# Splitting the first norm's squares, the first gating and the bias rows' skewed copies differently in a two-layer decoder trunk

## The chip, the core and the metric
One core of one Trainium2 chip runs the whole program. The metric is the device time of one execution in microseconds; three runs of the kernel before gave 973.3, 973.38 and 974.68, median 973.38.

## What is computed
Two layers over x of 256 positions by 1024 channels, all in float32. Each layer is: a SwiGLU feed-forward block (hidden width 2816) added at half weight, a mixer (differential attention with a relative bias, a short gated convolution, a gated linear recurrence), and a second half-weight SwiGLU block; each starts from an RMS norm.

```python
def rms_norm(x, g, eps=RMS_EPS):
    y = xf * lax.rsqrt(jnp.mean(xf * xf, axis=-1, keepdims=True) + eps)
    return y * g
def swiglu(x, w_gate, w_up, w_down):
    return (jax.nn.silu(x @ w_gate) * (x @ w_up)) @ w_down
for l in range(DEPTH):
    h = x + 0.5 * swiglu(rms_norm(x, ffn1_norm[l]), ffn1_gate[l], ffn1_up[l], ffn1_down[l])
    ...                       # mixer; its attention adds bias = rel_bias[t5_bucket(q - k)]
    x = h + 0.5 * swiglu(rms_norm(h, ffn2_norm[l]), ffn2_gate[l], ffn2_up[l], ffn2_down[l])
return rms_norm(x, final_norm)
```

## The kernel before
**Weights.** SP loads the weights in pieces of 512 KB (tile `raw`, 6 buffers, L151). Each piece is split in two parts for TensorE: ACT writes the high part `wh` (L162), DVE the rest `wl` (L166); there are 7 buffers of each, so at most 7 pieces are ready ahead of PE. The helper `pump()` splits the next piece, `take(n)` hands ready pieces to PE, and `done(n)` frees them and starts their loads.

**A feed-forward block.** `up_gate` walks 11 units of 256 hidden columns. A unit is four pieces; each piece gives two rows of blocks (`na` and `nb`, one for each half of the positions), in 12 matmuls of three kinds (L204, L205, L206: high by high, low by high, high by low). After its four pieces a unit is gated (`gate`): ACT applies Silu into `sg` (L315, two instructions, scaled by the norm's reciprocal root `norm.r`), DVE multiplies into `ga` (L317, two). The gated unit is turned (`turn`) after the second piece of the next unit: PE transposes it into `hT` (L326, four), ACT takes the high part into `hid` (L328), DVE the low part (L329). Then come the down pieces, for four blocks n of output channels, each six pieces of eight pairs of matmuls (L221, L222; the last piece half as many), accumulating over the hidden units in order: the first five pieces of a block need units 0 to 9, the next unit 10. The turn of the last unit (`last()`) stands after the second down piece (k0 == 4).

**The norm.** It is applied late: the matmuls run on x times its gain, and `norm.r` enters at the gating. `Norm.ssq` sums the squares in `xq` over partitions on PE (L249); `start` makes the mean on DVE (L237), the power on POOL (L241) and two scaled identity matrices `dg` on DVE (L244), which only the mixer's `spread` reads. In the very first block the squares come from x itself (`first_squares`: two ACT squares into `junk`, L807, then three POOL adds, L808 to L810), placed after unit 0; ssq and the gating of unit 0 come after the second piece of unit 1, its turn after the fourth.

**Work hidden in the first block.** A table of hooks runs small pieces of preparation after the units 1, 2, 4, 5, 6, 7 and 9: loads of constants, bias rows (`bias_rows`: one matmul, and a copy into `br`, 8 partitions by 384 values), exponents, a softplus polynomial, factors. `skew_out` (unit 7, L457) writes `br` to a DRAM tile `skew`, each of the 8 rows 128 times over: one DMA on ACT's queue of 1024 rows of 1536 bytes, 1.5 MB. `skew_in` (unit 9, L461) reads it back, shifted by one place for each partition, into `bias` (128 partitions by 8 by 256, 1 MB), again from ACT's queue; ACT waits at that instruction until the first transfer has landed. The instructions of an engine run in the order in which the program was written.

Of the kernel before, what the change touches and what calls it, by code (L numbers as in the profile page):

```python
# [11 lines left out]
F32 = mybir.dt.float32  # L12
F32R = mybir.dt.float32r
AF = mybir.ActivationFunctionType
ALU = mybir.AluOpType
AX = mybir.AxisListType

P = 128
DEPTH = 2
S = 256  # L20
# [32 lines left out]
UNITS = KF // 2  # L53
# [17 lines left out]
def trunk(ctx: ExitStack, tc: tile.TileContext, t, out):  # L71
    nc = tc.nc
# [4 lines left out]
    wk = ctx.enter_context(tc.tile_pool(name="wk", bufs=2))  # L77
    sm = ctx.enter_context(tc.tile_pool(name="sm", bufs=4))
    ps = ctx.enter_context(tc.tile_pool(name="ps", bufs=8, space=bass.MemoryType.PSUM))
    dr = ctx.enter_context(tc.tile_pool(name="dr", bufs=1, space=bass.MemoryType.DRAM))  # L80

    def bank(name):
        return ps.tile([P, 512], F32, tag="bank", name=name)

    def pair(name):
        return [bank(name + "a"), bank(name + "b")]
# [18 lines left out]
    xq = cst.tile([P, S], F32, name="xq")  # L105
    ident = cst.tile([P, P], F32, name="ident")
    ones = cst.tile([P, P], F32, name="ones")
    bd = cst.tile([P, 2, DEPTH * 2, P], F32, name="bd")
    bias = cst.tile([P, 8, S], F32, name="bias")
# [89 lines left out]
    def done(n):  # L199
        st["done"] += n  # L200
# [7 lines left out]
    def col(o, w, i, vh, vl, ks, first=0, last=KD - 1):  # L208

        c = slice(i * P, (i + 1) * P)  # L210
        for k in ks:
            wh, wl = w[k // 4]
            mm3(o, wh[:, k % 4, c], wl[:, k % 4, c], vh[:, k], vl[:, k], k == first, k == last)
# [10 lines left out]
    def tok(k):  # L224
        return slice(k * P, (k + 1) * P)
# [8 lines left out]
    class Norm:  # L234
        def start(self, ssq):
            ms = sm.tile([P, 2], F32, tag="ms", name="ms")
            nc.vector.tensor_scalar(  # L237
                out=ms, in0=ssq, scalar1=1.0 / D, scalar2=RMS_EPS, op0=ALU.mult, op1=ALU.add
            )
            self.r = sm.tile([P, 2], F32, tag="rr", name="rr")  # L240
            nc.gpsimd.tensor_tensor(out=self.r, in0=ms, in1=mhalf[:, :2], op=ALU.pow)  # L241
            self.dg = wk.tile([P, 2, P], F32, tag="dg", name="dg", bufs=1)
            for k in range(2):
                nc.vector.tensor_scalar_mul(out=self.dg[:, k], in0=ident, scalar1=self.r[:, k:k + 1])  # L244

        def ssq(self):
            b = bank("ssq")
            for k in range(2):
                nc.tensor.matmul(  # L249
                    b[:, k:k + 1], lhsT=xq[:, k * P:(k + 1) * P], rhs=ones[:, 0:1], start=True, stop=True  # L250
                )
            self.start(b[:, 0:2])

        def spread(self):
            b = bank("rb")
# [42 lines left out]
    def up_gate(norm, first, hooks=()):  # L298

        hooks = dict(hooks)  # L300
        hid, tiles = [], []
        for j, n in enumerate((10, 8, 4)):
            tile_ = big.tile([P, n, 2, S], F32R, tag=f"A{j}", name=f"hid{j}")
            tiles.append((len(hid), tile_))
            hid += [tile_[:, k] for k in range(n)]

        def hidden(c):
            k0, tile_ = [x for x in tiles if x[0] <= 2 * c][-1]
            return tile_[:, 2 * c - k0:2 * c - k0 + 2]

        def gate(b):
            s = wk.tile([P, 2, 256], F32, tag="sg", name="sg")
            a = wk.tile([P, 2, 256], F32, tag="ga", name="ga")
            for k in range(2):
                nc.scalar.activation(out=s[:, k], in_=b[k][:, :256], func=AF.Silu, scale=norm.r[:, k:k + 1])  # L315
            for k in range(2):
                nc.vector.scalar_tensor_tensor(  # L317
                    out=a[:, k], in0=b[k][:, 256:], scalar=norm.r[:, k:k + 1], in1=s[:, k], op0=ALU.mult, op1=ALU.mult
                )
            return a  # L320

        def turn(c, a):
            b = bank("hT")
            for j in range(2):
                for k in range(2):
                    nc.tensor.transpose(b[:, (2 * j + k) * P:(2 * j + k + 1) * P], a[:, k, tok(j)], ident)  # L326
            h = hidden(c)
            nc.scalar.activation(out=h[:, :, 0], in_=two(b), func=AF.Copy)  # L328
            nc.vector.tensor_tensor(out=h[:, :, 1], in0=two(b), in1=h[:, :, 0].bitcast(F32), op=ALU.subtract)  # L329

        late = {}
        for c in range(UNITS):
            b = pair("n")
            if first and c == 0:
                start(b)
                first_squares()
            else:
                for j in range(4):
                    w = [None] * j + take(1)
                    if j < 3 or c > 0:  # L340
                        for k in range(2):
                            rows(b[k], w, k, (2 * j, 2 * j + 1))
                    else:
                        for k in range(2):
                            rows(b[k], w, k, (KD - 2,))
                        rows(b[0], w, 0, (KD - 1,))
                        norm.ssq()
                        rows(b[1], w, 1, (KD - 1,))
                    done(1)
                    if first and c == 1:  # L350
                        if j == 1:
                            norm.ssq()
                            late[0] = gate(b0)
                        if j == 3:
                            turn(0, late.pop(0))
                    elif j == 1 and c > 0:
                        turn(c - 1, late.pop(c - 1))
                    pump()
            if first and c == 0:
                b0 = b  # L360
            else:
                late[c] = gate(b)
            if c in hooks:
                hooks[c]()
        return hid, lambda: turn(UNITS - 1, late.pop(UNITS - 1))

    def ffn(norm, first, gain, hooks=()):
        hid, last = up_gate(norm, first, hooks)
        for n in range(4):
            acc = pair("d")  # L370
            for k0, k1 in DOWN_K:
                w = take(1)[0]
                for i in range(2):
                    c = slice(i * P, (i + 1) * P)
                    for k in range(k0, k1):
                        wide(acc[i], w[0][:, k - k0, c], w[1][:, k - k0, c], hid[k], k == 0, k == KF - 1)
                    if k1 == KF:
                        settle(2 * n + i, acc[i], gain, True)
                done(1)
                if n == 0 and k0 == 4:  # L380
                    last()
                pump()


    kept = {}
# [66 lines left out]
        kept["br"] = wk.tile([8, 384], F32, tag="at", name="br")  # L452
        nc.vector.tensor_copy(out=kept["br"], in_=b[:8, :384])

    def skew_out():
        kept["skew"] = dr.tile([8, P, 384], F32, name="skew")
        nc.scalar.dma_start(out=kept["skew"], in_=kept["br"].unsqueeze(1).to_broadcast([8, P, 384]))  # L457

    def skew_in():
        sk = kept["skew"][:]  # L460
        nc.scalar.dma_start(  # L461
            out=bias, in_=bass.AP(sk.tensor, sk.offset + P - 1, [[383, P], [P * 384, 8], [1, S]])
        )


    def mixer(l, norm):
# [180 lines left out]
            col(lxb[i][:, :S], w, i, xh, xl, range(KD - 1))  # L647
        col(lxb[0][:, :S], w, 0, xh, xl, (KD - 1,))
        norm.ssq()
        col(lxb[1][:, :S], w, 1, xh, xl, (KD - 1,))  # L650
        done(2)
        pump()
# [44 lines left out]
        for i in range(2):  # L697
            j = 2 * l + i
# [30 lines left out]
        for i in range(2):  # L729
            nc.vector.tensor_tensor_scan(  # L730
                out=tv[:, i], data0=av[:, i], data1=bx[:, i], initial=0.0, op0=ALU.mult, op1=ALU.add
# [8 lines left out]
        for i in range(2):  # L740
            nc.scalar.activation(
                out=cs[:, i], in_=cp[:, i, 2:], func=AF.Copy, scale=par("sc_conv_w", l * 6 + 4 + i)
# [61 lines left out]
    def first_squares():  # L804
        junk = big.tile([P, KD, S], F32, tag="A3", name="junk")
        for i in range(2):
            nc.scalar.activation(out=junk[:, 4 * i:4 * i + 4], in_=xT[:, 4 * i:4 * i + 4], func=AF.Square)  # L807
        nc.gpsimd.tensor_tensor(out=junk[:, 0:4], in0=junk[:, 0:4], in1=junk[:, 4:8], op=ALU.add)  # L808
        nc.gpsimd.tensor_tensor(out=junk[:, 0:2], in0=junk[:, 0:2], in1=junk[:, 2:4], op=ALU.add)
        nc.gpsimd.tensor_tensor(out=xq, in0=junk[:, 0], in1=junk[:, 1], op=ALU.add)  # L810

    norm = Norm()
    ffn(norm, True, ("mix_norm", 0), {1: constants_in, 2: bias_rows, 4: exponents, 5: softplus, 6: factors, 7: skew_out, 9: skew_in})
    for l in range(DEPTH):
        norm = Norm()
        mixer(l, norm)
        norm = Norm()
        if l < DEPTH - 1:
            ffn(norm, False, ("ffn1_norm", l + 1))
            norm = Norm()  # L820
# [13 lines left out]
    hid, turn_last = up_gate(norm, False, {2 + 2 * k + n: turn_back(k, n) for k in range(2) for n in range(2)})  # L834
# [43 lines left out]
    for d in range(KF - 4):  # L878
        w = take(1)[0]
        for k in range(2):  # L880
            for n in range(len(cuts[k])):
                row(k, n, w, d)
        done(1)
        if d == 4:
            turn_last()
        pump()
    w = take(4)
# [54 lines left out]
```

## Time and profile before

| | us |
|---|---|
| three runs | 973.3, 973.38, 974.68 |
| the profiled execution | 973.29, of it span 971.3 |
| PE busy | 955.9 (98%) |
| DVE, ACT, POOL busy | 584.8, 507.2, 26.6 |
| share of PE in the chain that ended last | 92% |
| share of the `skew` write in it | 4% |

A row of the timeline has its start, its duration and what it is; in brackets stands how long the engine had been idle before it, and what released it. [...] Busy times overlap, so they are not to be added; a matmul of 512 columns is shown with 0.39 us, but one starts 0.2275 us after the other.

### The profile page before, as it was taken

Reading aid. Unit: us, or ns where it says so; the run is one execution under the profiler, and the core shown is the slowest. Engines: PE = TensorE matmul, PEld = TensorE weight load, DVE = VectorE, ACT = ScalarE, POOL = GpSimd, SP = SyncE. Lnnn points to the kernel's source line nnn. Section 1 sums busy time; section 2 is a strip of 40 time slices with the busy share of each in tenths; the row PEclk is TensorE's granted clock in tenths of the full one; section 3 lists DMA queues with packets and bytes.
Section 4 is the critical chain, followed back from the end, with each engine's and each line's share of the span. In section 5 each row is a group of like instructions: output and inputs, shape, how many; then the busy total and the mean of one; then the engine's idle time right before and its main releaser. Section 6 shows DMA issues by size and latency. Waiting matters only on the chain.

```text
span 971.3 us, 13926 instructions
## 1 busy us (share of the span) xinstructions
PE 955.9 (98%) x5350; PEld 831.4 (86%) x5350; DVE 584.8 (60%) x817; ACT 507.2 (52%) x775; POOL 26.6 (3%) x49
## 2 busy tenths in 40 slices
PE   8899999999999999999999999999999999999997
PEld 7688877899999888888888888888999988888886
DVE  5666536667787555556655555565678765555543
ACT  6555435457775544444544445454678554444431
POOL 2003000000000000000000000000000000000000
PEclk9999999999999999999999999999999999999999
DMA  8575667554356555546555555556445465555531
GB/s 305 191 242 197 149 176 268 189 174 152 131 177 214 193 192 180 188 158 197 183 202 176 176 192 184 182 167 218 160 135 164 161 214 190 178 175 191 191 117 44
DMA packets 52997, 176.64 MB, mean 182 GB/s; under 512 B 6819, under 2 KB 8900, under 8 KB 52932
## 3 DMA queue, kind: packets, MB, share of 16 engines
q1 hardware_dynamic: 48960, 171.46, 51.8%
q10 hardware_dynamic: 3972, 4.29, 2.0%
q8 instruction: 42, 0.69, 0.3%
q14 instruction: 23, 0.19, 0.1%
HBM read 173.11 MB, written 2.62 MB: 181 GB/s over the span
## 4 chain that ended last, share of the span: by engine, by line
PE 92%; DMA 4%; ACT 1%; DVE 1%; issue 1%; SPq 0%; POOL 0%; ACTq 0%; POOLq 0%; DVEq 0%
PE na L205 8%; PE nb L204 8%; PE na L206 8%; PE nb L205 8%; PE nb L206 8%; PE na L204 8%; PE da L221 6%; PE db L221 6%; DMA skew<-br 4%; PE da L222 3%; PE db L222 3%; PE hT L326 2%; PE v L204 1%; PE wb L206 1%; PE wb L205 1%
## 5 line engine op out<-in xcount | busy, mean ns | idle before, releaser
L162 ACT ACTIVATE wh<-raw 128x1024 fp32r<-128x1024 f32 (+1 forms) x334 | 339.6, 1030 | 277.0 <-PE nb L206 106.9
L166 DVE TENSOR_TENSOR wl<-raw,wh 128x1024 fp32r<-128x1024 f32 (+1 forms) x334 | 390.8, 1194 | 80.0 <-ACT wh L162 80.0
L205 PE MATMUL na<-wl,xx 128*128 128x512 f32 x352 | 137.7, 391 | 4.8 <-DVE wl L166 4.8
L204 PE MATMUL na<-wh,xx 128*128 128x512 f32 x352 | 141.5, 402 | 0.5 <-ACT wh L162 0.5
L204 PE MATMUL nb<-wh,xx 128*128 128x512 f32 x352 | 137.9, 392 | 0.0
L206 PE MATMUL na<-wh,xx 128*128 128x512 f32 x352 | 137.7, 391 | 0.0
L206 PE MATMUL nb<-wh,xx 128*128 128x512 f32 x352 | 137.5, 391 | 0.0
L205 PE MATMUL nb<-wl,xx 128*128 128x512 f32 x352 | 137.5, 390 | 0.0
L329 DVE TENSOR_TENSOR hid<-hT,hid 128x512 fp32r<-128x512 f32 x44 | 30.4, 692 | 128.4 <-ACT hid L328 128.4
L221 PE MATMUL da<-hid,wh 128*128 128x512 f32 x252 | 93.6, 403 | 0.0
L221 PE MATMUL db<-hid,wh 128*128 128x512 f32 x252 | 92.3, 399 | 0.0
L205 PEld LDWEIGHTS na<-wl,xx 128*128 128x128 f32 x352 | 66.3, 188 | 18.0 <-DVE wl L166 5.9
L206 PEld LDWEIGHTS nb<-wh,xx 128*128 128x128 f32 x352 | 66.4, 189 | 14.1
L205 PEld LDWEIGHTS nb<-wl,xx 128*128 128x128 f32 x352 | 66.4, 189 | 14.0
L204 PEld LDWEIGHTS nb<-wh,xx 128*128 128x128 f32 x352 | 66.4, 189 | 14.0
L206 PEld LDWEIGHTS na<-wh,xx 128*128 128x128 f32 x352 | 66.2, 188 | 14.1
L204 PEld LDWEIGHTS na<-wh,xx 128*128 128x128 f32 x352 | 66.3, 188 | 13.4 <-ACT wh L162 1.4
L328 ACT ACTIVATE hid<-hT 128x512 fp32r<-128x512 f32 x44 | 26.2, 596 | 89.4 <-PE hT L326 89.4
L222 PE MATMUL da<-hid,wl 128*128 128x256 f32 x252 | 71.3, 283 | 0.0
L222 PE MATMUL db<-hid,wl 128*128 128x256 f32 x252 | 70.7, 281 | 0.0
L317 DVE SCALAR_TENSOR_TENSOR ga<-na,rr,sg 128x256 f32<-128x256 f32 x44 | 21.2, 483 | 73.8 <-ACT sg L315 73.8
L221 PEld LDWEIGHTS da<-hid,wh 128*128 128x128 f32 x252 | 47.9, 190 | 11.2
(283 smaller groups left out, 1523.2 us busy)
## 6 DMA issues: line engine op xcount, KB each, us to landing
raw<-in_ffn_gu SPq DMA_DIRECT2D x172, 512.0 KB, 4.4
raw<-in_ffn_down SPq DMA_DIRECT2D x82, 512.0 KB, 4.4
raw<-in_w_in SPq DMA_DIRECT2D x44, 512.0 KB, 4.6
raw<-in_w_out SPq DMA_DIRECT2D x16, 512.0 KB, 4.9
raw<-in_ffn_down SPq DMA_DIRECT2D x12, 256.0 KB, 2.7
raw<-in_ffn_gu SPq DMA_DIRECT2D x8, 256.0 KB, 5.0
skew<-br ACTq DMA_DIRECT2D x1, 1536.0 KB
xT<-in_x SPq DMA_DIRECT2D x4, 256.0 KB, 5.4
```

The source lines that it names most:

```text
L162: nc.scalar.activation(out=parts[i][0][:, s], in_=raws[i][:, s], func=AF.Copy)
L166: nc.vector.tensor_tensor(out=lo[:, s], in0=raws[i][:, s], in1=h[:, s].bitcast(F32), op=ALU.subtract)
L204: nc.tensor.matmul(o, lhsT=ah, rhs=bh, start=first, stop=False)
L205: nc.tensor.matmul(o, lhsT=ah, rhs=bl, start=False, stop=False)
L206: nc.tensor.matmul(o, lhsT=al, rhs=bh, start=False, stop=last)
L221: nc.tensor.matmul(o, lhsT=wh, rhs=flat(v), start=first, stop=False)
L222: nc.tensor.matmul(o[:, :S], lhsT=wl, rhs=v[:, 0], start=False, stop=False)
L317: nc.vector.scalar_tensor_tensor(out=a[:, k], in0=b[k][:, 256:], scalar=norm.r[:, k:k + 1], in1=s[:, k], op0=ALU.mult, op1=ALU.mult)
L326: nc.tensor.transpose(b[:, (2 * j + k) * P:(2 * j + k + 1) * P], a[:, k, tok(j)], ident)
L328: nc.scalar.activation(out=h[:, :, 0], in_=two(b), func=AF.Copy)
L329: nc.vector.tensor_tensor(out=h[:, :, 1], in0=two(b), in1=h[:, :, 0].bitcast(F32), op=ALU.subtract)
```

## The change
Four things are moved. (1) `first_squares` goes from after unit 0 to the second piece of unit 1, and its three adds from POOL to DVE. (2) ssq goes to after the first piece of unit 2; units 0 and 1 are gated together after its second piece, and gated units stand in a queue from which each later piece but a unit's first turns one (so unit 0 in unit 2 after the third piece, unit 1 after the fourth, later units after the second piece of the next unit as before). The last turn of a block goes from the second down piece to the third. (3) `dg` is made in the mixer only. (4) Exponents, softplus and factors run one unit earlier, and the skewed copies are cut into four parts of two partitions: out(i) at unit 6+i for i = 0 to 3 (256 rows of 1536 bytes, 393 KB), followed at the same unit by in(i-1) (256 KB), so in(0) to in(3) at the units 7 to 10.

```diff
@@ class Norm: start @@
-            self.dg = wk.tile([P, 2, P], F32, tag="dg", name="dg", bufs=1)
-            for k in range(2):
-                nc.vector.tensor_scalar_mul(out=self.dg[:, k], in0=ident, scalar1=self.r[:, k:k + 1])
...
+        def diagonal(self):
...
@@ up_gate @@
-        late = {}
+        gated, banks = [], []
+
+        def turn_next():
+            if gated:
+                turn(*gated.pop(0))
+
         for c in range(UNITS):
             b = pair("n")
+            banks.append((c, b))
             if first and c == 0:
                 start(b)
-                first_squares()
             else:
...
                     done(1)
-                    if first and c == 1:
-                        if j == 1:
-                            norm.ssq()
-                            late[0] = gate(b0)
-                        if j == 3:
-                            turn(0, late.pop(0))
-                    elif j == 1 and c > 0:
-                        turn(c - 1, late.pop(c - 1))
+                    if first and c == 1 and j == 1:
+                        first_squares()
+                    if first and c == 2 and j == 0:
+                        norm.ssq()
+                    if j > 0:
+                        turn_next()
                     pump()
-            if first and c == 0:
-                b0 = b
-            else:
-                late[c] = gate(b)
+                    if first and c == 2 and j == 1:
+                        gated += [(i, gate(o)) for i, o in banks[:2]]
+                        banks = banks[2:]
+            if not first or c > 1:
+                gated += [(i, gate(o)) for i, o in banks]
+                banks = []
...
@@ ffn; the final block has the same with d @@
-                if n == 0 and k0 == 4:
+                if n == 0 and k0 == 8:
                     last()
...
-    def skew_out():
-        kept["skew"] = dr.tile([8, P, 384], F32, name="skew")
-        nc.scalar.dma_start(out=kept["skew"], in_=kept["br"].unsqueeze(1).to_broadcast([8, P, 384]))
-
-    def skew_in():
+    def skew_out(i):
+
+        if i == 0:
+            kept["skew"] = dr.tile([8, P, 384], F32, name="skew")
+        m = slice(2 * i, 2 * i + 2)
+        rows_ = kept["br"][m].unsqueeze(1).to_broadcast([2, P, 384])
+        nc.scalar.dma_start(out=kept["skew"][m], in_=rows_)
+
+    def skew_in(i):
...
+    def skew(i):
+        def go():
+            if i < 4:
+                skew_out(i)
+            if i > 0:
+                skew_in(i - 1)
+        return go
...
-        nc.gpsimd.tensor_tensor(out=junk[:, 0:4], in0=junk[:, 0:4], in1=junk[:, 4:8], op=ALU.add)
-        nc.gpsimd.tensor_tensor(out=junk[:, 0:2], in0=junk[:, 0:2], in1=junk[:, 2:4], op=ALU.add)
-        nc.gpsimd.tensor_tensor(out=xq, in0=junk[:, 0], in1=junk[:, 1], op=ALU.add)
+        for n in (4, 2):
+            nc.vector.tensor_tensor(out=junk[:, 0:n], in0=junk[:, 0:n], in1=junk[:, n:2 * n], op=ALU.add)
+        nc.vector.tensor_tensor(out=xq, in0=junk[:, 0], in1=junk[:, 1], op=ALU.add)
...
-    ffn(norm, True, ("mix_norm", 0), {1: constants_in, 2: bias_rows, 4: exponents, 5: softplus, 6: factors, 7: skew_out, 9: skew_in})
+    once = {1: constants_in, 2: bias_rows, 3: exponents, 4: softplus, 5: factors}
+    ffn(norm, True, ("mix_norm", 0), once | {6 + i: skew(i) for i in range(5)})
```

What the change makes of the order on ACT around the first gating. `whN` is the high part of piece N (unit c has the pieces 4c to 4c+3), `sg` a Silu. Before:

```order
L807 ACTIVATE junk_234<-xT_87 128x1024 x2
L162 ACTIVATE wh4_242<-raw4_111 128x1024
L162 ACTIVATE wh5_260<-raw5_113 128x1024
L162 ACTIVATE wh6_263<-raw6_160 128x1024
L315 ACT_TABLE_LOAD
L315 ACTIVATE sg_291<-na_126,rr_286 128x256
L315 ACTIVATE sg_291<-nb_127,rr_286 128x256
L162 ACTIVATE wh7_297<-raw7_184 128x1024
```

And now, from the squares to the first turn; wh16 is the piece whose buffer comes free when PE has used piece 9, unit 2's second:

```order
L162 ACTIVATE wh6_257<-raw6_160 128x1024
L828 ACTIVATE junk_275<-xT_87 128x1024 x2
L162 ACTIVATE wh7_281<-raw7_184 128x1024
...
L162 ACTIVATE wh16_404<-raw16_333 128x1024
L317 ACT_TABLE_LOAD
L317 ACTIVATE sg_410<-na_126,rr_372 128x256
L317 ACTIVATE sg_410<-nb_127,rr_372 128x256
L317 ACTIVATE sg_416<-na_234,rr_372 128x256
L317 ACTIVATE sg_416<-nb_235,rr_372 128x256
L330 ACTIVATE hid0_123<-hT_434 128x2x256
```

Before, the gating stood ahead of wh7, so of a piece of unit 1; now it stands behind wh16, and the squares behind wh6.

The second place is ACT at the skewed copies. Before, `skew` is written once, in the ACT order between the gating of unit 7 and wh39, and this is what stands around the read, from the gating of unit 9 on (`hid2` is the unit turned next):

```order
L315 ACTIVATE sg_1135<-na_1054,rr_286 128x256
L315 ACTIVATE sg_1135<-nb_1055,rr_286 128x256
L461 DMA bias_93<-skew_965 128x8x256
L162 ACTIVATE wh47_1156<-raw47_1046 128x1024
L328 ACTIVATE hid2_125<-hT_1174 128x2x256
L162 ACTIVATE wh48_1181<-raw48_1072 128x1024
```

Now, first around the gating of unit 7 to the gating of unit 8 (out(1) and in(0)):

```order
L317 ACTIVATE sg_958<-nb_878,rr_372 128x256
L468 DMA skew_875<-br_480 256x1x384
L472 DMA bias_93<-skew_875 128x2x256
L162 ACTIVATE wh39_980<-raw39_867 128x1024
L330 ACTIVATE hid1_124<-hT_998 128x2x256
L162 ACTIVATE wh40_1005<-raw40_895 128x1024
L162 ACTIVATE wh41_1023<-raw41_920 128x1024
L162 ACTIVATE wh42_1041<-raw42_938 128x1024
L317 ACTIVATE sg_1047<-na_966,rr_372 128x256
```

and behind the gating of unit 10, where the last read in(3) stands:

```order
L317 ACTIVATE sg_1225<-nb_1145,rr_372 128x256
L472 DMA bias_93<-skew_875 128x2x256
L162 ACTIVATE wh51_1250<-raw51_1134 128x1024
L162 ACTIVATE wh52_1272<-raw52_1162 128x1024
L330 ACTIVATE hid2_125<-hT_1294 128x2x256
```

Each of the four reads now stands between a gating and the splitting of the next pieces, and the next gating and the next `hid` stand behind it.

## Rows read from the trace of the kernel before

**Rows 1.** The page's head and its busy time by engine (us, share of the span, instructions).

```profile
span 971.3 us, 13926 instructions
PE 955.9 (98%) x5350; PEld 831.4 (86%) x5350; DVE 584.8 (60%) x817; ACT 507.2 (52%) x775; POOL 26.6 (3%) x49
```

**Rows 2.** The windows of 10 us: stretch, its length, busy time of PE, PEld, DVE, ACT and POOL (with instructions), granted TensorE clock, share of the DMA engines, GB/s.

```profile
20.00:30.00 10.00, 6.33 (x29) 5.00 (x28) 5.42 (x9) 4.51 (x6) 2.97 (x3) 0.96 0.32 106
30.00:40.00 10.00, 10.00 (x41) 8.10 (x41) 5.11 (x7) 3.33 (x6) 0.00 (x0) 0.87 0.76 246
...
60.00:70.00 10.00, 10.00 (x47) 8.28 (x47) 5.39 (x7) 5.25 (x7) 0.00 (x0) 1.00 0.54 187
...
140.00:150.00 10.00, 8.05 (x42) 6.64 (x42) 5.47 (x7) 6.11 (x9) 0.00 (x0) 0.93 0.77 269
150.00:160.00 10.00, 10.00 (x53) 8.64 (x53) 5.49 (x6) 3.82 (x5) 0.00 (x0) 0.90 0.89 308
```

**Rows 3.** The timeline of all engines from the squares to the start of unit 2 (start, duration, what, idle before and releaser).

```profile
15.04 2.40 POOL L808 TENSOR_TENSOR junk<-junk 128x1024 f32<-128x1024 f32 x1 [13.70 <-ACT junk L807]
...
15.94 4.81 DVE L166 TENSOR_TENSOR wl<-raw,wh 128x1024 fp32r<-128x1024 f32 x2 [1.97 <-ACT wh L162]
...
17.24 0.39 PE L204 MATMUL na<-wh,xx 128*128 128x512 f32 x1
...
18.58 0.50 PE L205 MATMUL na<-wl,xx 128*128 128x512 f32 x1 [0.95 <-DVE wl L166]
...
23.97 0.50 PE L249 MATMUL ssq<-ones,xq 128*128 128x1 f32 x4
...
24.33 0.48 PE L204 MATMUL na<-wh,xx 128*128 128x512 f32 x1
...
25.49 0.47 ACT L315 ACTIVATE sg<-na,rr 128x256 f32<-128x256 f32 x1 [6.39 <-POOL rr L241]
...
28.48 0.50 PE L205 MATMUL na<-wl,xx 128*128 128x512 f32 x1 [3.67 <-DVE wl L166]
...
31.06 0.63 PE L206 MATMUL nb<-wh,xx 128*128 128x512 f32 x1
...
35.81 0.48 PE L204 MATMUL na<-wh,xx 128*128 128x512 f32 x1
```

**Rows 4.** The same view around the turns of units 9 and 10.

```profile
132.91 0.39 PE L206 MATMUL nb<-wh,xx 128*128 128x512 f32 x1
...
134.25 0.94 PE L326 MATMUL hT<-ident,ga 128*128 128x128 f32 x4 [0.95 <-DVE ga L317]
...
134.94 0.47 PE L204 MATMUL na<-wh,xx 128*128 128x512 f32 x1
...
142.62 1.06 ACT L162 ACTIVATE wh<-raw 128x1024 fp32r<-128x1024 f32 x1 [8.58 <-DMA skew<-br]
...
146.03 0.28 PE L222 MATMUL db<-hid,wl 128*128 128x256 f32 x1
...
148.20 1.28 PE L326 MATMUL hT<-ident,ga 128*128 128x128 f32 x4 [1.89 <-DVE ga L317]
...
152.30 0.40 PE L221 MATMUL db<-hid,wh 128*128 128x512 f32 x1
```

**Rows 5.** The chain that ended last, in order of time (start, share of the chain's time, what).

```profile
76.55 0.43 PE hT L326 x4
...
87.90 0.44 PE hT L326 x4
...
105.32 36.70 DMA skew<-br
142.04 0.45 ACTq L461
...
176.81 0.24 PE da L221
...
179.64 0.23 PE da L221
```

**Rows 6.** The windows of two stretches of the first block, columns as in Rows 2: one with weight loads alone, and one with nearly nothing but the `skew` write.

```profile
60.00:100.00 40.00, 40.00 (x186) 33.13 (x186) 23.09 (x42) 22.14 (x30) 7.34 (x18) 1.00 0.57 190
112.00:114.00 2.00, 2.00 (x10) 1.64 (x9) 2.00 (x3) 0.75 (x2) 0.00 (x0) 1.00 0.43 48
```

**Rows 7.** The page's row of that DMA (size of one; its time to landing is in Rows 5).

```profile
skew<-br ACTq DMA_DIRECT2D x1, 1536.0 KB
```

**Rows 8.** The page's groups of instructions (busy us, mean ns of one, idle of the engine before them).

```profile
L166 DVE TENSOR_TENSOR wl<-raw,wh 128x1024 fp32r<-128x1024 f32 (+1 forms) x334 | 390.8, 1194 | 80.0 <-ACT wh L162 80.0
...
L329 DVE TENSOR_TENSOR hid<-hT,hid 128x512 fp32r<-128x512 f32 x44 | 30.4, 692 | 128.4 <-ACT hid L328 128.4
...
L328 ACT ACTIVATE hid<-hT 128x512 fp32r<-128x512 f32 x44 | 26.2, 596 | 89.4 <-PE hT L326 89.4
```

**Rows 9.** The timeline of ACT and DVE: four splits in a row, a table load, and the first and the last instruction of a gating.

```profile
46.38 3.89 ACT L162 ACTIVATE wh<-raw 128x1024 fp32r<-128x1024 f32 x4
...
73.00 1.28 ACT L419 ACT_TABLE_LOAD   x1
...
117.56 0.46 ACT L315 ACTIVATE sg<-na,rr 128x256 f32<-128x256 f32 x1
...
118.45 0.47 DVE L317 SCALAR_TENSOR_TENSOR ga<-nb,rr,sg 128x256 f32<-128x256 f32 x1
```

More of the change, by code (lines that the diff above doesn't have):

```diff
@@ L252, in ssq @@
             self.start(b[:, 0:2])
+        def diagonal(self):
+            self.dg = wk.tile([P, 2, P], F32, tag="dg", name="dg", bufs=1)
+            for k in range(2):
+                nc.vector.tensor_scalar_mul(out=self.dg[:, k], in0=ident, scalar1=self.r[:, k:k + 1])
         def spread(self):
@@ L349, in up_gate @@
                     done(1)
-                    if first and c == 1:
-                        if j == 1:
-                            norm.ssq()
-                            late[0] = gate(b0)
-                        if j == 3:
-                            turn(0, late.pop(0))
-                    elif j == 1 and c > 0:
-                        turn(c - 1, late.pop(c - 1))
-                    pump()
-            if first and c == 0:
-                b0 = b
-            else:
-                late[c] = gate(b)
+                    if first and c == 1 and j == 1:
[4 more added lines that the diff above has]
+                        turn_next()
+                    pump()
+                    if first and c == 2 and j == 1:
[4 more added lines that the diff above has]
+                banks = []
             if c in hooks:
                 hooks[c]()
-        return hid, lambda: turn(UNITS - 1, late.pop(UNITS - 1))
+        return hid, turn_next
     def ffn(norm, first, gain, hooks=()):
@@ L453, in bias_rows @@
         nc.vector.tensor_copy(out=kept["br"], in_=b[:8, :384])
-    def skew_out():
-        kept["skew"] = dr.tile([8, P, 384], F32, name="skew")
-        nc.scalar.dma_start(out=kept["skew"], in_=kept["br"].unsqueeze(1).to_broadcast([8, P, 384]))
-    def skew_in():
+    def skew_out(i):
[5 more added lines that the diff above has]
+    def skew_in(i):
         sk = kept["skew"][:]
         nc.scalar.dma_start(
-            out=bias, in_=bass.AP(sk.tensor, sk.offset + P - 1, [[383, P], [P * 384, 8], [1, S]])
-        )
+            out=bias[:, 2 * i:2 * i + 2],
+            in_=bass.AP(sk.tensor, sk.offset + 2 * i * P * 384 + P - 1, [[383, P], [P * 384, 2], [1, S]]),
+        )
+    def skew(i):
[5 more added lines that the diff above has]
+        return go
     def mixer(l, norm):
@@ L649, in mixer @@
         norm.ssq()
+        norm.diagonal()
         col(lxb[1][:, :S], w, 1, xh, xl, (KD - 1,))
@@ L883, in trunk @@
         done(1)
-        if d == 4:
+        if d == 8:
             turn_last()
```

## The prediction, made before the changed kernel had run

> **What bounds the kernel.** The page's head comes first: PE is busy in 98% of the span, DVE in 60%, ACT in 52% [rows 1]. So time can be won only where PE stands still or runs slowly, and the windows say where that is: PE fills nearly every 10 us at full clock, as in [rows 2] at 60 to 70, except at 20 to 40 and at 130 to 160. There it is idle, and the granted clock falls to 0.87 and 0.90 in the window after. Everything that the change touches lies in these two places.
>
> The timeline gives the first [rows 3]. Unit 1 begins at 17.24 and unit 2 at 35.81, 18.57 us. Undisturbed, a unit is 11.35 us from turn to turn (87.90 - 76.55, [rows 5]), turn included; ssq adds 0.36 (24.33 - 23.97). So 18.57 - 11.71 = **6.86 us** are lost. First PE waits for a `wl` at 18.58, while DVE takes 2.4 us for each split beside POOL's adds, against 1.19 elsewhere [rows 8]. Then ACT's Silu stands 6.39 us behind the norm's root, and all splits behind it, so that PE gets its next `wl` at 28.48. The clock is slow after that stop: 31.06 shows a matmul of 0.63 us, and 23 matmuls and a turn, 5.58 us at full pace (0.2275 apart, turn 0.35), take 35.81 - 28.48 = 7.33, so 1.75 of the loss is clock.
>
> The second place [rows 4]: the last matmul before unit 9's turn should end its turn of 0.2275 at 133.14, the turn starts at 134.25 and the next matmul at 134.94, which is 1.11 + 0.34 = 1.45 lost. Then ACT stands 8.58 us behind the `skew` write, released at 142.62; unit 10's turn wants to start at 146.15 and starts at 148.20, and until 152.30 the clock is slow: five pairs and a turn (5 x 0.354 + 0.35 = 2.12; a pair is 1/8 of 179.64 - 176.81, [rows 5]) take 4.10. Together 2.05 + 1.98 = 4.03. The place loses **5.48**.
>
> **The change, step by step.** *Squares.* POOL's adds go, and with them, I take it, the slow splits; DVE gets adds of 128x1024, x512 and x256, by the split's 1.19 for the first and a half and a quarter plus a fixed part for the rest some 2.3 us. They stand behind wl5 and ahead of wl6; ACT's squares (4 us) have moved behind wh6, so wh4 comes earlier. wl6 is needed at 17.24 + 5.5 = 22.7 and ends near 22.3: nothing, with 0.4 us of cover. If it is gone, each us late costs one.
>
> *ssq and gating.* ssq now has a whole piece, 2.75 us, before the gating needs its root. The gating stands behind wh16, whose buffer comes free with unit 2's second piece; from there ACT and DVE need 0.97 + 1.28 (table load) + 1.36 (118.92 - 117.56) = 3.61 [rows 9], and the turn comes 2.75 later: **0.9 lost**. From below it is nothing, if wh16 goes before the table load costs anything (the load may be hidden in ACT's wait for the buffer); from above 4.1, if the seven loads of constants, which ACT now issues ahead of wh13 (0.45 each, [rows 5]), have no cover left: 0.9 + 3.2. Net gain here 6.86 - 0.9 = 5.96. The two `dg` instructions and the hooks moved a unit earlier lie on DVE and POOL with room [rows 2]: nothing.
>
> *Last turn a piece later.* It gives unit 10's gating 2.84 us more; its `hid` is needed at the sixth down piece, three pieces on. Free by itself.
>
> *The skewed copies.* If no read makes ACT wait, all 5.48 is won: then 973.29 - 5.96 - 5.48 = 961.85. The order shows what decides it: ACT meets out(i), then in(i-1), which waits for out(i-1), and the next gating and `hid` stand behind. The whole write took 36.70 us [rows 5] for 1024 x 1536 bytes [rows 7]. Where it runs nearly alone it moves 48 GB/s with a DMA share of 0.43 [rows 6]: 6.9 of 16 engines, so about one for each of its eight partitions, at 7.0 GB/s each. At that rate the bytes take 32.8, and 3.9 are fixed. A part has two partitions, hence two engines, for 393 KB. No row shows two engines at this; the bounds are these. Weight loads reach 190 GB/s on 0.57 x 16 = 9.1 engines [rows 6], 20.8 each: 9.4 us a part if two engines don't hinder each other (8.2 if a part kept the whole's 48 GB/s). At 7.0 each it is 28.1. Eight of them sharing something makes the low rate partly theirs, and the loads beside them slow both; I take the middle, **s = 18.7 us**, since neither row is nearer: the one is the same kind of transfer with four times the sharers, the other has no small reads of one partition.
>
> [...]
>
> Now the chain, with 0 at the end of unit 6, parts behind one another on the same engines: part i has landed at s + 3.9 + i s. Behind in(i-1) ACT needs four splits, a `hid` and a gating, 3.89 + 0.60 + 1.36 = 5.9 [rows 8, 9], until the next turn can start. The turns want to start at 28.13 (unit 8: two units, two pieces), 39.48 (unit 9), 53.9 (unit 10: four units, three down pieces). Behind in(3), two splits and both halves of `hid`, 1.95 + 0.60 + 0.69 = 3.3, are due with the sixth down piece at 59.95. With s = 18.7 these are ready at 28.5, 47.2, 65.9 and 82.0, so PE has stood 0.4, 7.7, 12.0 and in the end **22.05 us** (4 s - 52.75). Three of the four stops (7.3, 4.3, 10.0) are longer than the 1.89 of [rows 4] after which the clock fell, and cost (1.75 + 1.98) / 2 = 1.87 each: **5.6**. The 0.95 stops were followed by no such fall.
>
> Issuing seven more DMAs takes ACT 7 x 0.45 = 3.2 us, spread over five units in which it is half idle: nothing.
>
> **The sum.** 961.85 + 22.05 + 5.6 = **989.5**. The profiled execution, 973.29, is 0.09 from the median, so nothing is to be converted. The case's own range: s = 16 gives 11.25 and two falls (2.3 and 7.3; the third stop is 1.6), 976.8, and s = 21 gives 31.25 and four falls (7.5), 1000.6.
>
> **Rivals.** *A: the parts are quick* (the other side, faster). Up to s = 13.2 no read holds PE, and the time is **962**. Its place is the wait of in(3); it decides at s = 15.6, where 9.65 of stops and one fall, 1.87, eat the 11.44. For it: the 20.8 GB/s of an engine in weight loads, and bounds that start at 8.2; against: the write's 7.0 where hardly anything else was on the DMA engines. A quarter of the chance.
>
> *B: the parts don't gain from being fewer*, s = 28.1: 4 x 28.1 - 52.75 = 59.7, four falls 7.5, so **1029**. For it: 7.0 is the only measured rate of this transfer. Against: raw loads beside them are not slowed like that.
>
> *C: the parts overlap*, each on other engines with 18.7 of its own. The reads then end some 11.35 apart or where ACT issues the next write, unit 10's turn is 2.7 late and the last `hid` 5.9, two falls: 961.85 + 5.9 + 3.7 = **971.5**. Against it: nothing in the trace says that two small writes would choose different engines.
>
> **Chances.** Forecast 0.60, A 0.25, B 0.07, C 0.05, and 0.03 for an s at the balance point. A measurement tells 0.2% (1.9 us) from no change. Faster is A and C, 0.30; the same 0.03; slower the forecast and B, 0.67. The range takes in A and the forecast: from 960.9 (A with no wait at the first turn, 973.29 - 6.86 - 5.48) to 1000.6; it leaves out B and the tail above s = 21. The forecast's own range is 977 to 1000.6.
>
> **What would show it.** Right: unit 1 takes 11.4 us and unit 2 some 12.6, at full clock from 17 to 50; the writes land about 23, 41, 60 and 79 us after the first issue; ACT's longest idle times name them; PE waits before the turns of units 9 and 10 and before the sixth down piece, each followed by slow matmuls. Wrong: landing times under 16 us apart, or reads of which ACT's waits show nothing; or a first turn several us late, which would be the constants' loads.

## The result, and the profile after

The changed kernel takes 978.88 us (median of four runs, 978.68 to 980.97) against 973.71 for the kernel before beside it: ratio 1.0057, interval 1.0039 to 1.0074. A second study gave 978.99 and 1.0056 (1.0039 to 1.0073). It is slower, as forecast, but by 5.2 us (5.8 in the second study) and not by 16.

The page's head, and its row of the four writes:

```profile
span 976.5 us, 13921 instructions
...
PE 955.3 (98%) x5350; PEld 830.9 (85%) x5350; DVE 581.4 (60%) x812; ACT 506.7 (52%) x775; POOL 24.1 (2%) x46
...
skew<-br ACTq DMA_DIRECT2D x4, 384.0 KB
```

PE does the same work as in [rows 1], so the 5.2 us of span are waits and clock. The windows, columns as in [rows 2], say where:

```profile
0.00:10.00 10.00, 7.30 (x27) 6.11 (x28) 4.55 (x10) 6.07 (x12) 1.63 (x8) 0.87 0.79 266
...
20.00:30.00 10.00, 10.00 (x46) 8.29 (x45) 8.37 (x10) 4.92 (x6) 0.00 (x0) 1.00 0.73 251
30.00:40.00 10.00, 9.17 (x43) 7.26 (x41) 5.54 (x8) 6.64 (x9) 1.56 (x1) 1.00 0.98 291
...
130.00:140.00 10.00, 2.49 (x11) 1.72 (x10) 4.17 (x5) 5.10 (x7) 0.00 (x0) 0.85 0.50 146
140.00:150.00 10.00, 9.63 (x39) 7.96 (x40) 1.84 (x3) 0.00 (x0) 0.00 (x0) 0.81 0.58 178
```

The hole at 20 to 30 is gone, and a much larger one stands at 130 to 140. PE's timeline has the turns by which to count (start, duration, idle before):

```profile
39.80 0.85 PE L328 MATMUL hT<-ident,ga 128*128 128x128 f32 x4 [0.83 <-DVE ga L319]
...
95.50 0.60 PE L328 MATMUL hT<-ident,ga 128*128 128x128 f32 x4
...
106.86 0.60 PE L328 MATMUL hT<-ident,ga 128*128 128x128 f32 x4
...
120.63 0.94 PE L328 MATMUL hT<-ident,ga 128*128 128x128 f32 x4 [2.27 <-DVE ga L319]
...
140.37 1.29 PE L328 MATMUL hT<-ident,ga 128*128 128x128 f32 x4 [7.88 <-DVE ga L319]
...
156.53 0.77 PE L328 MATMUL hT<-ident,ga 128*128 128x128 f32 x4
...
164.40 0.50 PE L221 MATMUL da<-hid,wh 128*128 128x512 f32 x1 [1.54 <-DVE hid L331]
```

Unit 6's turn (95.50) comes 3.6 us earlier than before:

```profile
99.09 0.60 PE L326 MATMUL hT<-ident,ga 128*128 128x128 f32 x4
```

That row is of the kernel before. From unit 6's turn the sixth down piece is due 54.49 later (59.95 - 5.46), at 149.99, and starts at 164.40: **14.4 lost**, where the kernel before lost 5.48. So -3.6 + 14.4 - 5.5 = +5.3, which is the span's 5.2.

ACT's timeline over the four parts (rows with ACTq are its queue's issues; the second number is how long one took):

```profile
90.38 0.75 ACTq L468 DMA_DIRECT2D skew<-br  x1
...
101.73 0.67 ACTq L468 DMA_DIRECT2D skew<-br  x1
...
112.31 2.10 ACTq L472 DMA_DIRECT2D bias<-skew  x1
...
115.03 1.46 ACTq L468 DMA_DIRECT2D skew<-br  x1
...
127.35 6.80 ACTq L472 DMA_DIRECT2D bias<-skew  x1
134.25 1.06 ACT L162 ACTIVATE wh<-raw 128x1024 fp32r<-128x1024 f32 x1 [14.63 <-issue]
134.77 1.61 ACTq L468 DMA_DIRECT2D skew<-br  x1
...
143.68 7.00 ACTq L472 DMA_DIRECT2D bias<-skew  x1
...
160.62 0.39 ACTq L472 DMA_DIRECT2D bias<-skew  x1
```

A read is issued when its write has landed: 21.9, 37.0, 53.3 and 70.2 us after the first write's issue, so 15.0, 16.3 and 16.9 apart. And the issue itself holds ACT: 2.1, 6.8 and 7.0 us where another write is on the queue, 0.39 where none is.

### The profile page after: what moved, and what is told of

Read it like the earlier page. It is cut to its first block, busy times and chain, and to the rows that moved or that the text cites. A ratio compares the mean times of both kernels' runs of the same rounds, so it can differ in the third digit from the quotient of the medians.

```text
span 976.5 us, 13921 instructions
## 1 busy us (share of the span) xinstructions
PE 955.3 (98%) x5350; PEld 830.9 (85%) x5350; DVE 581.4 (60%) x812; ACT 506.7 (52%) x775; POOL 24.1 (2%) x46
## 4 chain that ended last, share of the span: by engine, by line
PE 91%; DMA 6%; issue 1%; ACT 1%; ACTq 0%; DVE 0%; POOLq 0%; POOL 0%; SPq 0%
PE nb L204 8%; PE na L206 8%; PE na L204 8%; PE na L205 8%; PE nb L206 8%; PE nb L205 8%; PE da L221 6%; PE db L221 6%; DMA skew<-br 5%; PE da L222 3%; PE db L222 3%; PE hT L328 2%; PE v L204 1%; PE q L205 1%; PE wb L205 1%; PE wb L204 1%
```

## The experiments

**One piece again.** The changed kernel with the whole write at unit 7 and the whole read at unit 9.

```diff
...
-    ffn(norm, True, ("mix_norm", 0), once | {6 + i: skew(i) for i in range(5)})
+    ffn(norm, True, ("mix_norm", 0), once | {7: skew_out, 9: skew_in})
```

> The changed kernel with the skewed copy in one piece again (write at unit 7, read at unit 9, as before). Theory (the cut copies are the loss, the rest of the change works): the first units gain the 5.96 of the prediction, unit 10's turn, now a piece later, no longer waits (before lost 4.03 there), unit 9's 1.45 stays: 973.3 - 10.0 = 963.3; with a slow start like the one in the changed kernel's trace (first matmul 0.4 later and nine matmuls at 0.43 instead of 0.23) 965.5. Rival (the new gating or the start is what costs): 973 or more.

965.25 us, ratio 0.9910 (0.9898 to 0.9923). The rest of the change is worth 8.9 us, and the cut turns that into a loss.

**The cut alone.** The kernel before with only the copy cut in four.

> The kernel before with nothing changed but the skewed copy, cut in four as in the change (units 6 to 10). Theory: the last read comes 70 us after the first write and its followers 4.2 later, where PE wants them at 60, so PE loses 14.4 in place of the 5.5 it lost: 973.4 + 8.9 = 982.3, up to 984 if the earlier last turn adds a fall of the clock. Rival (the gating part is the loss): 973.4.

984.48, ratio 1.0109 (1.0096 to 1.0122): 10.4 us lost. So the cut is the loss. The two don't add up (-8.9 + 10.4 is 1.5, not 5.2). A likely reason, which no run takes apart: the later last turn wins less where a later wait sets the end.

**The reads on POOL's queue.**

```diff
-        nc.scalar.dma_start(
+        nc.gpsimd.dma_start(
             out=bias[:, 2 * i:2 * i + 2],
```

> The changed kernel with the four reads issued from POOL's queue in place of ACT's; the writes stay where they are. Theory (the loss is ACT standing behind the writes): ACT never waits for them, the parts take their 15 us and more as before, and nobody waits: 962 to 966 (the upper end with the slow start). Rival (the two busy engines starve the weight loads): ACT then waits for raw instead, over 970. Rival (the write itself becomes quicker or slower when the reads are on another queue): the landing times in the trace tell.

975.21, ratio 1.0013 (1.0003 to 1.0022). Only 3.7 us come back. ACT waits for no write any more, but for `raw` (22.7 us for the down pieces), and PE still stands. SP's queue does too, as the waits of SP and of PE from 85 to 175 say (what was waited for: us in total, times, longest):

```profile
SPq L151 <- DMA skew<-br: 32.7, 3, 12.3
...
PE da L221 <- DVE hid L331: 7.0, 1, 7.0
```

That ACT's place behind the reads is the whole loss, my theory, is refuted: the weight loads suffer too.

**Other pairs of partitions.** 0 and 4, 1 and 5, 2 and 6, 3 and 7; the same rows and bytes.

```diff
-        m = slice(2 * i, 2 * i + 2)
+        m = slice(i, i + 5, 4)
...
```

> The changed kernel with other pairs of partitions in the four parts: 0 and 4, 1 and 5, 2 and 6, 3 and 7, the same bytes and rows. Port theory (two neighbouring partitions share one way out of SBUF): a part takes 8 to 10 us instead of 15 to 17, no read holds PE, 962 to 966. Engine theory (two engines carry a part and set its time whatever the partitions): parts 15 to 17 us apart as before, 978 to 980.

965.27, ratio 0.9915 (0.9902 to 0.9929): 13.6 us better than the change, by a choice of partitions. ACT's queue there (the first and the second write were issued at 90.00 and 101.36):

```profile
107.69 1.50 ACTq L472 DMA_DIRECT2D bias<-skew  x1
...
116.73 6.51 ACTq L472 DMA_DIRECT2D bias<-skew  x1
```

The first part lands after 17.7 and the second 9.0 behind it (in the change: 21.9 and 15.0). The later two land 17.4 and 19.0 us after their own issue, not 8 to 10, but no PE row waits for one. The last lands 53.0 after the first issue, which is an s of 12.3, under the 13.2 up to which the prediction had no read holding PE. The trace's records of the write's single packets of 1536 bytes (1024 of them in each run) show the difference; their median durations:

```
kernel before, eight partitions, 0 to 7        216 ns
the change, pairs 0-1, 2-3, 4-5, 6-7           108 ns   (47% of them 65, most others 105 to 120)
far pairs                                       65 ns
128 partitions, below                           65 ns
```

So the median packet takes 216 ns where eight neighbours are read, 108 where two are, and 65 where the two lie four apart: neighbours slow each other, as the port theory expects. How they do it no run shows. One way out for both does not explain every packet: in the change, from 112.87 to 113.44, two packets of a neighbouring pair are under way nearly all the time, and each takes 65. The packets are not the whole spacing either: the 128 of one engine make 11.6 us at the change's mean of 91 ns and 8.3 at 65, while the parts land 15.0 to 16.9 and 9.0 to 13.4 apart.

That a part has two engines shows in a stretch of the change, 124 to 126, where the DMA share is 0.12, so 1.9 of 16 (columns as in [rows 6]). Of these 3.8 us the write's packets fill 2.2, and the rest are packets of weight loads and of in(0); no more than two packets of any kind are under way at once, but for 0.06 us:

```profile
124.00:126.00 2.00, 2.00 (x11) 1.65 (x10) 0.00 (x0) 0.00 (x0) 0.00 (x0) 1.00 0.12 35
```

Weight loads beside a write land late: here by the change's DMA page from 91 to 119 and the kernel before's from 100 to 120 (KB each, median us to landing). With no write beside them they took 3.9 (that row stands with the run on POOL's queue).

```profile
raw<-in_ffn_gu SPq DMA_DIRECT2D x4, 512.0 KB, 8.4
```

```profile
raw<-in_ffn_down SPq DMA_DIRECT2D x4, 512.0 KB, 16.9
```

**Constants behind the first gating**, on top of the far pairs.

```diff
-    once = {1: constants_in, 2: bias_rows, 3: exponents, 4: softplus, 5: factors}
+    once = {2: constants_in, 3: lambda: (bias_rows(), exponents()), 4: softplus, 5: factors}
```

> The kernel with the far pairs of partitions (0 and 4, 1 and 5, ...), and the loads of constants moved from unit 1 to unit 2, so behind the first gating on ACT, bias rows to unit 3. There the first turn stood 2.03 us and, in some executions, the clock fell after it. Theory (ACT's 6.5 us of issuing seven loads ahead of wh13 makes the first turn late): the first turn waits 0.3 to 0.9, the time falls by 1.2 to 2.5 to 962.8 to 964. Rival (the wait is the table load and the gating behind wh16 alone): 2 us of wait and 965.3 as before.

963.83, ratio 0.9904 (0.9887 to 0.9921), and the first turn waits 0.84 where it waited 2.03 with the far pairs alone (here the row of this run, then that of the far pairs). That is the 0.9 of the sum without the constants. The gain in time, 1.4 us, is not clear of noise: the two intervals overlap.

```profile
38.13 0.85 PE L328 MATMUL hT<-ident,ga 128*128 128x128 f32 x4 [0.84 <-DVE ga L319]
```

```profile
39.42 0.85 PE L328 MATMUL hT<-ident,ga 128*128 128x128 f32 x4 [2.03 <-DVE ga L319]
```

**The writes early**, units 3 to 6, the reads left at 7 to 10.

> The changed kernel with its four writes moved three units earlier (units 3 to 6) and the reads left at units 7 to 10, so that no read meets a write that is under way. Theory (the loss is ACT standing behind the writes, in the reads and in their issue): 964 to 966. Rival (the slow writes hurt the weight loads too, SP waiting for them or the two engines being shared): ACT waits for raw in the units 3 to 7 instead and the time lies between 967 and 976, as it did with the reads on POOL's queue (975.2).

978.00, ratio 1.0053 (1.0034 to 1.0071): nothing is won. But the run does not do what it was meant to do. Parts that landed 15.0 to 16.9 us apart in the change, issued 8 to 11 apart here, pile up, and the last write's packets run until 129.8, past the first read. No read waits for a landing any more; instead ACT is held in the issues themselves (90.18 is the fourth write, 107.23 the first read), and SP's queue waits (50 to 175). So this run does not part what ACT loses from what the loads lose.

```profile
SPq L151 <- DMA skew<-br: 35.9, 3, 12.4
```

```profile
90.18 6.82 ACTq L468 DMA_DIRECT2D skew<-br  x1
...
107.23 9.37 ACTq L472 DMA_DIRECT2D bias<-skew  x1
```

In the change's trace the issues of the weight loads and of ACT's transfers carry the same eight semaphores in turn, and SP waits 20.3 us for `skew` (85 to 175). The load issued at 127.39 carries the semaphore of the write that landed at 127.35.

**Writes and reads on POOL's queue**, with neighbouring pairs as in the change.

> The changed kernel with both the four writes and the four reads issued from POOL's queue (neighbouring pairs as in the change). What stays of the loss with the reads alone on POOL (975.2) is to be told apart. Theory (SP waits for a write because its weight loads and ACT's transfers take the same eight completion semaphores in turn): POOL's transfers have their own, SP no longer waits for skew, 962 to 966. Rival (a weight load shares engines and the port with the write and is itself late): ACT waits for raw and the time is 970 to 976.

993.52, ratio 1.0212 (1.0195 to 1.0230). SP waits for no `skew` from 25 to 190 (in the change 20.3 us), and the run is 14.6 us worse than the change. The rival's sign shows (ACT waits 36.9 us for `raw` from 85 to 175), though the time lies far over its 970 to 976. The weight loads themselves are late, by the DMA page of the stretch 86 to 119 of this run, and then of 60 to 100 of the kernel before (KB each, median us to landing):

```profile
raw<-in_ffn_gu SPq DMA_DIRECT2D x8, 512.0 KB, 24.0
skew<-br POOLq DMA_DIRECT2D x1, 384.0 KB, 39.8
```

```profile
raw<-in_ffn_gu SPq DMA_DIRECT2D x13, 512.0 KB, 3.9
```

But the edit changes more than what SP waits for. Nothing holds POOL, so it issues the first two writes together, and they land 34.5 and 39.8 us later; the later two meet each other as well:

```profile
84.43 2.39 POOL L468 DMA_DIRECT2D skew<-br  x2
```

From this queue the bytes go in 336 packets of 4608, with three or four under way for most of the time, where ACT's queue has 1024 of 1536 and never more than two (but for 0.9 of 67 us). How much of the 24.0 comes from the two writes at once, how much from the larger packets, and how much from SP no longer holding its loads back, no run takes apart; nor does one show what the loads share with the write.

**The last turn early again** (k0 == 4), otherwise the change.

> The changed kernel with a block's last turn at the second down piece again, as in the kernel before. Theory (the chain of writes sets the end, and the turn only has to wait for the gating behind in(2)): unit 10's turn now waits some 2 us for its gating, the clock falls after it, and PE comes later to the sixth down piece than the 164.4 of the changed kernel: 979 to 982. Rival (the turn's place was worth a whole piece): 978.9 + 2.84 and a fall of the clock, over 983.

982.22, ratio 1.0086 (1.0065 to 1.0107). Unit 10's turn waits 2.66 us there, and the clock is low behind it (0.72 from 154 to 160). The later place is worth some 3 us; the interval reaches over the rival's 983, so the time alone does not exclude it.

**128 partitions.** The bias rows repeated 16 times on 128 partitions, one write at unit 7, one read at unit 9.

```diff
-        nc.tensor.matmul(b[:8, :384], lhsT=kept["rb"], rhs=kept["oneh"], start=True, stop=True)
+        rb16 = sm.tile([NB + 1, 8, 16], F32, tag="rb16", name="rb16", bufs=1)
+        nc.vector.tensor_copy(out=rb16, in_=kept["rb"].unsqueeze(2).to_broadcast([NB + 1, 8, 16]))
+        nc.tensor.matmul(b[:, :384], lhsT=rb16.rearrange("p h r -> p (h r)"), rhs=kept["oneh"], start=True, stop=True)
...
+            out=kept["skew"].rearrange("h (r q) n -> (h r) q n", q=8),
+            in_=kept["br"].unsqueeze(1).to_broadcast([P, 8, 384]),
...
```

> The skewed copy in one piece (write at unit 7, read at unit 9) but from bias rows that stand on 128 partitions, each head 16 times (DVE repeats the 33 x 8 table 16 times along its columns ahead of the one matmul, and the copy to SBUF is 128 wide). Port theory (a write's time goes with the ports its partitions lie behind): the 1.5 MB land in about 12 us instead of 36.7, SP and ACT never wait for them, unit 9's turn is on time; 963.5 to 965, a little below the one-piece write from eight partitions (965.25). Rival (the DRAM side limits the write): it still lands after 30 us or more and the time is 965.3.

971.33, ratio 0.9987 (0.9974 to 1.0000): the write is as expected (9.6 us; the 12 was my estimate), the time isn't. The write's row, and what else PE met:

```profile
skew<-br ACTq DMA_DIRECT2D x1, 1536.0 KB, 9.6
```

```profile
43.33 0.60 PE L328 MATMUL hT<-ident,ga 128*128 128x128 f32 x4
47.43 1.62 PE L460 MATMUL bt<-oneh,rb 33*128 33x384 f32 x2 [3.50 <-issue]
48.98 0.79 PE L204 MATMUL na<-wh,xx 128*128 128x512 f32 x1
49.57 0.63 PE L205 MATMUL na<-wl,xx 128*128 128x512 f32 x1
```

1.5 MB land in 9.6 us instead of 36.7. But the 16-fold table is made on DVE right ahead of its matmul (at 47.12, behind a gating), PE stands 3.5 us for it, and matmuls of 0.63 us follow: a wait that my edit brought in.

**All of it mended.** 128 partitions, that table made in unit 4 and its matmul in unit 6, constants at unit 2, the first gating ahead of wh15 and wh16.

> The best of what the runs showed: bias rows on 128 partitions and the skewed copy in one piece (units 7 and 9), the 16-fold table made in unit 4 and the matmul in unit 6 so that PE doesn't wait for it (3.5 us and a fall of the clock in the one-piece run), constants loaded at unit 2, and the first gating ahead of wh15 and wh16. Theory (all losses of the changed kernel are the narrow write, the constants and the splits ahead of the first gating): nothing left in the first 150 us but the start, 973.5 - 6.9 - 5.5 = 961.1, at most 963. Rival (the first turn is held by something else): 963.8 or more, as with the constants moved.

961.33 (960.98 to 961.57), ratio 0.9877 (0.9862 to 0.9892), 12 us better than the kernel before and 17.6 better than the change. After its first two matmuls PE waits for nothing up to 200 us; all that it waited for there:

```profile
PE warm L805 <- DVE ones L797: 1.0, 1, 1.0
PE na L204 <- ACT wh L162: 0.6, 1, 0.6
PE na L205 <- DVE wl L166: 0.2, 1, 0.2
```

**The change once more.**

> The changed kernel once more, for a second profile. Its first profile began 0.4 us late with nine slow matmuls, 2.2 us lost, and its first turn waited only 0.83. If that start was of the one execution, this one starts at 5.7, its first turn waits 2.0 to 2.3, and the time is again 978 to 980; if it is of the kernel, it shows again.

978.99. The start is ordinary (5.69), and the first turn waits 3.25 us, more than expected:

```profile
40.19 1.20 PE L328 MATMUL hT<-ident,ga 128*128 128x128 f32 x4 [3.25 <-DVE ga L319]
```

```profile
29.85 3.86 ACTq L407 DMA_DIRECT2D bd<-in_lru_wx  x2
33.84 3.90 ACT L162 ACTIVATE wh<-raw 128x1024 fp32r<-128x1024 f32 x4 [6.61 <-DMA bd<-in_lru_wa]
37.76 1.28 ACT L317 ACT_TABLE_LOAD   x1
```

In this execution ACT takes from 26.18 to 33.71 to issue the seven loads, then come four splits, the table load and the gating. Unit 6's turn stands at 97.26, 1.8 us before its time in the kernel before, and the sixth down piece at 166.39, 14.6 after it is due: 14.6 - 5.5 - 1.8 = 7.3, and the span, 978.5, is 7.2 longer. So the late start of the first profile was of that one execution, and what it cost it also hid, in a shorter wait of the first turn.

## Why the prediction was right and wrong

The direction, the two places and the mechanism (parts one after another, and PE behind them) were right; the size was wrong, 16 us for 5.2. Three terms failed: a part's time s (18.7, where the last landing gives 16.6), the falls of the clock added on top of the stops (5.6, where they cost nothing at the end), and the issues of the constants' loads, taken as covered.

**What bounds the kernel, and the two places**: right. The mended kernel takes 961.3; the sum had 960.9 with no wait for the copies and none at the first turn.

**Squares, ssq, gating, `dg`, hooks**: right in kind. No split is slow beside the squares (three take 3.49 us from 21.48), and from 20 to 30 us PE is full. (ACT's two squares take 2.0 us together, not 4; nothing hung on it.) The net gain was 3.6 and 1.8 in the two profiles, not 5.96. The failing term is the cover of the constants' loads: 3.2 us of issues at 0.45 each, set to nothing in the sum, were 6.3 and 7.5 us on ACT. The bound from above, 4.1, held the 3.25 measured, and with the loads moved the wait was the sum's 0.9. In the second profile the clock fell after that wait as well (four matmuls of 0.63 us from 41.62, where later ones take 0.39); in the first, 2.2 us went to the late start. The 0.45 was read from the one read of `bias`. The loads' own issues in the kernel before run from 36.32 to 43.89, and ACT stands 4.68 us for them there:

```profile
36.32 0.34 ACTq L390 DMA_DIRECT2D lamv<-in_lams  x1
...
42.61 1.28 ACTq L400 DMA_DIRECT2D bd<-in_lru_wx  x2
43.99 2.01 ACT L162 ACTIVATE wh<-raw 128x1024 fp32r<-128x1024 f32 x2 [4.68 <-issue]
```

**The parts**: two engines, one part after the other, and ACT held by the reads were right; s = 18.7 was too long. Spacings of 15.0 to 16.9 were measured. That the parts go behind one another on the same engines was an assumption that no run before the change shows; in the change no more than two of the write's packets are under way at once, but for 0.9 of 67 us. The middle between 9.4 and 28.1 was not the way to choose: with two neighbours in place of eight the median packet took 108 ns in place of 216, so an engine moved 14 GB/s and not the 7.0 of [rows 6], and by that, an estimate, 393 KB take 14 us. The last `hid` came 74.4 us after unit 6's end and not 82.0: 7.6 too much.

**More issues on ACT** (six, which the prediction counts as seven), 3.2 us and nothing in the sum, were 19.5 us: 20.8 for the eight, 1.3 for the two before. The read at 127.35 alone took 6.8, so unit 9's turn came at 140.4 and not 5.9 behind the landing, at 133.3. Here it cost nothing, because the last write set the end.

**The falls of the clock**: 5.6 on top of the stops was a wrong step. The end was set by a transfer; what PE lost to a slow clock after the turn of unit 9 was lost inside the time in which it would have waited anyway, and unit 10's turn, with a stop of 4.3 forecast, waited for nothing. In this place only a fall after the last stop adds to the time, and after 1.54 us none came (granted 1.00 from 164.4 to 170). Nor did each stop longer than 1.89 bring a fall: after the 2.27 of unit 8's turn and the 2.03 of the far pairs' first turn the clock stayed full (1.00 from 121 to 125, and from 40 to 50), after 3.25 matmuls took 0.63 us, and after 7.88 the clock was low (0.81 from 140 to 150).

So 16.2 - 7.6 - 5.6 + 2.4 = 5.4, of 5.2 in the first profile; with the second's 7.4 and 4.1 it is 7.3, of 7.2.

**Who waits**: incomplete. The prediction had ACT alone behind the writes. With the reads on POOL's queue 975 us remain, because SP's loads stand behind the write (32.7 us; in the change itself 20.3, with the far pairs 6.9) and, in the change, land late beside it (8.4 in place of 3.9). What is shown is that parts whose two partitions lie four apart take the loss away, whoever waits (965.3). How much of the change's 14.4 is ACT and how much the loads is not shown.

**Rivals**: A's premise, quick parts, is what the far pairs are, and its price was right to 3.3 us. B and C are refuted: 15 to 17 us a part and not 28 (though weight loads beside the write are slowed, contrary to what stood against B: 16.9 us in the kernel before, 3.9 without one); and the write's packets run no more than two at a time (but for 0.9 of 67 us), so the parts do not overlap.

## What to carry to other kernels

Price a transfer from a few neighbouring partitions by a measured packet, at the number of neighbours that are read at once (here 216 ns with eight, 108 with two, 65 with two that lie four apart). Cutting it into neighbouring pairs won nothing here: it cost 10.4 us by itself, and in the change the parts landed 15.0 to 16.9 us apart. Pairs four apart landed 9.0 to 13.4 us apart, and the whole, spread over 128 partitions, took 9.6 us instead of 36.7. So try those two before splitting. The slow transfer had three kinds of victims here: the engine that waits for it, the next issues on its queue (up to 7.0 us in the change, in place of 0.39), and the weight loads beside it (8.4 us in place of 3.9); moving the first out of the way showed the others (975.2, where the theory had 962 to 966). Where a chain of transfers set the end, the stops ahead of it and the slow clock between them were not to be added: the 5.6 us of the forecast cost nothing.

## What the runs showed that I had not expected

An issue on ACT's queue took 0.39 us with nothing ahead of it and as much as 6.8, 7.0 and 9.37 us behind a narrow write that was still under way (2.1 behind another). The same eight partitions' rows, spread over 128, landed in 9.6 us instead of 36.7. And writes for which neither SP nor ACT waited, from POOL's queue and two at a time, cost more than any other placing: weight loads of 24.0 us instead of 3.9, and 993.5 us in all.
